# A two-layer attention backbone: transposes in place of diagonal products in the opening, six buffers for the modulation weights, and the opening left to the scheduler's order

## The chip, the cores and the metric

One NeuronCore of a Trainium2 chip; the other cores are not used. The metric is the device time of one execution in microseconds (us), the median of three runs.

The engines are called by the names of the profile: PE is TensorE (PEld its loading of weights), DVE is VectorE, ACT is ScalarE, POOL is GpSimd, and SP is the engine whose queue issues nearly all DMA transfers. Each engine takes its instructions in the order in which they stand in its own queue, and waits on semaphores for the others.

## The reference

One sequence of 1024 tokens `x` and 256 context tokens `ctx`, 1024 wide, in float32, go through two layers: windowed attention with sink logits, then multi-head latent attention. What matters here is the start of layer 0:

```
for i in range(DEPTH):
    shift_x, scale_x, gate_x = adaln(c, ada_w[i], ada_b[i])        # silu(cond) @ ada_w + bias, split in 3
    shift_c, scale_c, gate_c = adaln(c_ctx, ada_w[i], ada_b[i])
    hx = rms_norm(x, norm_g[i]) * (1.0 + scale_x[:, None]) + shift_x[:, None]
    hc = rms_norm(ctx, norm_g[i]) * (1.0 + scale_c) + shift_c
    ...
    q, k, v, g = jnp.split(h @ w_in, [...], axis=-1)               # layer 0, for hx and hc
    ...                                                            # attention, gate, output projection
    x = x + gate_x[:, None] * yx
return rms_norm(x, final_g)
```

So before the first projection can start, the modulation (shift and scale) must be computed from `ada_w`, 8 MB of it in this layer, every row of `x` and `ctx` must be normalised, and the result must stand with the channels on the partitions, since a product on PE sums over partitions.

## The kernel before

**Number format.** A float32 value is split into a high part (`hi`, rounded to the format that PE reads in one pass) and a low part (`lo = src - hi`); `split` makes both, the high part on ACT and the low part on DVE or POOL. A product is three matmuls (`mm3`, L126 to L128): high x high, low x high, high x low.

**Tiles.** The 1280 tokens (context first) are ten tiles of 128 rows (`x_load(i)`, i = 0 to 9), or five pairs p of 256. `h` is held transposed, `hT[p]`, channels on partitions: 8 chunks of 128 channels, high and low.

**The opening** (L656 to L856) does the following before the loop of projections.

- `ada_load(h, k)` (L671) loads 128 rows of `ada_w` for half h of the columns (512 of shift, 512 of scale): sixteen loads of 512 KB, through the ring of buffers `awr`. `ada_mm(h, k)` (L675) multiplies such a piece with `silu(c)` and sums in PSUM bank `PA`: two products with only two rows of output. `ada_cols(h)` copies the sums out (L678, on ACT), turns them into columns (L680) and adds bias and gain (L168, L171).
- `norm(i)`: sum of squares of a tile on ACT (L691), then mean, epsilon and the power -1/2 on POOL (L692, L693).
- `diag(i)` (L699, on DVE): a 128 x 128 diagonal matrix with the reciprocal root of each row.
- `turn(g)` (L711, on PE): a group g is one pair p and two of its 8 chunks (`parts[g]`; 20 groups, the first eight alternate between pairs 0 and 1). Four products of a 128 x 128 piece of the raw tile with the diagonal give the scaled piece, transposed, in one of four PSUM banks. In the profile each of these float32 products is two records.
- `h_part(g)`: modulation out of PSUM on DVE (L722, two instructions) and the high part on ACT (L723); `h_low(g)`: the low part on POOL or DVE (L728).
- `v_part(g)`: 12 matmuls (4 products) with the V columns of `w_in`, into `PB[:, 4 + p % 2]`; after the last group of a pair the V rows are stored (L744, L746).
- `w0_load`, `w0_cut`: the load (L752) and the split of the 1 MB of V columns. `fetch(1)` starts the next block of weights (L288), `cosa` and `sina` are loaded (L851, L852).

**What sets the order.** Before the opening the framework's scheduler orders each engine's queue by its own estimate of when an instruction can run. `tc.manual_schedule()` stops that: from where it is entered to where it is left, every queue has the order of the source. In the kernel before it is entered ahead of the opening, so opening and projections are in source order. In both kernels it is left behind the projections; the attention of layer 0 and layer 1 are ordered by the scheduler.

**Rings.** A `Ring` hands out the buffers of a list in turn. A load into a buffer waits until those that read its former content are done, and everything behind it in SP's queue waits with it.

**After the opening**: ten blocks of 256 columns of `w_in` for all tokens (`proj_t`), with the rest of the modulation computed on DVE beside it (`ada_vec`, L342 and L344, its pieces loaded at L323), then attention by units, output projection, and layer 1.

Of the kernel before, what the change touches and what calls it, by code (L numbers as in the profile page):

```python
# [12 lines left out]
AF = mybir.ActivationFunctionType  # L13
# [10 lines left out]
NP = TOK // 256  # L24
# [35 lines left out]
def kernel(ctx: ExitStack, tc: tile.TileContext, t, out, dbg=None):  # L60
# [591 lines left out]

    awr = Ring(F, [0, 4, 8, 12], 1024)
    xs = Ring(F, [16, 20, 24, 28], 1024)  # L656
    w0 = f_at(32, 8, 256)
    am = f_at(40, 512)
    dg = Ring(F, [42, 42.5, 43, 43.5], 128)
    junk = f_at(50, 512).bitcast(BF16)  # L660
    hr = Ring(F, [44, 46, 48, 32], 512)
    PA, PM = PB[:, 6, :], PB[:, 7, :]
    parts = [(p, b) for h in range(2) for p in range(2) for b in (2 * h, 2 * h + 1)]
    parts += [(p, b) for p in range(2, NP) for b in range(4)]
    NG = len(parts)
    aw, xn, hs = {}, {}, {}

    def ada_load(h, k):
        aw[h, k] = shp(awr.next(), 2, 512)
        src = t["ada_w"][0, k * 128 : k * 128 + 128, 0 : 2 * D].rearrange("p (a c) -> p a c", a=2)  # L670
        load(out=aw[h, k], in_=src[:, :, h * 512 : h * 512 + 512])  # L671

    def ada_mm(h, k):
        for a in range(2):
            nc.tensor.matmul(PA[32 * a : 32 * a + 2], sc[:, k, :], aw[h, k][:, a, :], start=k == 0, stop=k == 7)  # L675
# [9 lines left out]
    def x_load(i):  # L685
        xn[i] = [xs.next(), sm_ring()]
        load(out=xn[i][0], in_=src0(i))

    def norm(i):
        st = xn[i][1]  # L690
        nc.scalar.activation(junk, xn[i][0], AF.Square, accum_out=st[:, 0:1])  # L691
        nc.gpsimd.tensor_scalar(st[:, 1:2], st[:, 0:1], 1.0 / D, EPS, ALU.mult, ALU.add)  # L692
        nc.gpsimd.tensor_tensor(st[:, 2:3], st[:, 1:2], mhalf, ALU.pow)  # L693

    def diag(i):

        st = xn[i][1]
        xn[i][1] = dg.next()
        nc.vector.tensor_scalar_mul(xn[i][1], ident, st[:, 2:3])  # L699

    def bank(g):
        return shp(PB[:, g % 4, :], 2, 256)

    def turn(g):

        p, b = parts[g]
        for kk in range(2):
            for j in range(2):
                x, d = xn[2 * p + j]
                c0 = (2 * b + kk) * 128  # L710
                nc.tensor.matmul(  # L711
                    bank(g)[:, kk, j * 128 : j * 128 + 128], x[:, c0 : c0 + 128], d, start=True, stop=True
                )

    def h_part(g):
        p, b = parts[g]
        w = 1 if p == 0 else 0
        hs[g] = shp(hr.next(), 2, 256)
        for kk in range(2):
            k = 2 * b + kk  # L720
            sa, sb = ada0.A[:, k, w : w + 1], ada0.B[:, k, w : w + 1]
            nc.vector.tensor_scalar(hs[g][:, kk], bank(g)[:, kk], sa, sb, ALU.mult, ALU.add)  # L722
        nc.scalar.copy(hT[p][:, 0, 2 * b : 2 * b + 2, :], hs[g])  # L723
# [24 lines left out]
    wt[0] = r_at(wst[0], 2, 8, 256)  # L748

    def w0_load(i):  # L750
        ks = slice(4 * i, 4 * i + 4)
        load(out=w0[:, ks, :], in_=w_in[512 * i : 512 * i + 512, 1280:1536].rearrange("(k p) n -> p k n", p=128))  # L752

    def w0_cut(i):
        ks = slice(2 * i, 2 * i + 2)
        split(wt[0][:, 0, ks, :], wt[0][:, 1, ks, :], w0[:, ks, :], nc.vector if i % 2 else nc.gpsimd)


    in_order = tc.manual_schedule()
    in_order.__enter__()  # L760
    nc.vector.memset(PA[0:34], 0.0)
    ada_load(0, 0)
    load_small()
# [2 lines left out]
    x_load(0)  # L766
    x_load(1)
    ada_load(0, 3)
    ada_mm(0, 0)
    ada_load(0, 4)  # L770
    ada_mm(0, 1)
    ada_load(0, 5)
    w0_load(0)
    ada_mm(0, 2)
    ada_load(0, 6)
    for i in range(2):
        norm(i)
    for i in range(2):
        diag(i)
    ada_mm(0, 3)  # L780
    ada_load(0, 7)
    w0_cut(0)
    w0_cut(1)
    ada_mm(0, 4)
    ada_mm(0, 5)
    x_load(2)
    x_load(3)
    turn(0)
    turn(1)
    ada_mm(0, 6)  # L790
    ada_mm(0, 7)
    ada_load(1, 0)
    w0_load(1)
    for k in (1, 2, 3):
        ada_load(1, k)
    ada_cols(0)
    norm(2)
    h_part(0)
    norm(3)
    h_part(1)  # L800
    diag(2)
    diag(3)
    h_low(0, nc.gpsimd)
    turn(2)
    turn(3)
    ada_mm(1, 0)
    ada_load(1, 4)
    for g in (2, 3):
        h_part(g)
        h_low(g - 1, nc.gpsimd)  # L810
        turn(g + 2)
        v_part(g - 2)
        ada_mm(1, g - 1)
        ada_load(1, g + 3)
    h_low(3, nc.vector)
    turn(6)
    turn(7)
    v_part(2)
    ada_mm(1, 3)
    ada_load(1, 7)  # L820
    for i in range(4, 8):
        x_load(i)
    w0_cut(2)
    w0_cut(3)
    v_part(3)
    for k in range(4, 8):
        ada_mm(1, k)
    ada_cols(1)
    for g in range(4, NG + 2):
        if g < NG:  # L830
            h_part(g)
        p = (g + 4) // 4
        if g % 4 < 2 and p < NP:
            norm(2 * p + g % 4)
        if g % 4 == 2 and p < NP:
            diag(2 * p)
            diag(2 * p + 1)
        if 5 <= g <= NG:
            h_low(g - 1, nc.vector if g % 4 == 0 else nc.gpsimd)
        if 6 <= g < NG - 2:  # L840
            turn(g + 2)
        if g == 8:
            next_item()
            fetch(1)
        if g == 9:
            x_load(8)
            x_load(9)
        if g in (11, 13, 15):
            next_item()
        if g == 12:  # L850
            load(out=cosa, in_=t["cos_a"])  # L851
# [792 lines left out]
```

## Time and profile before

| | us |
|---|---|
| median of 3 runs | 1653.48 (1653.24 to 1655.42) |
| the profiled execution | 1653.19 |
| its span, first to last instruction | 1651.1 |
| PE busy | 1587.6 |
| DVE, ACT, POOL busy | 944.9, 802.0, 813.3 |
| first matmul | 6.22 |
| first h_part (L722) | 24.50 |
| last wait of the V product in the opening, ended at | 105.68 |

A matmul's row in the timeline is its start, its length with the drain behind it, the line and the shape; matmuls overlap, so the time that one takes from the next is the distance between two starts. What stands in brackets at the end of a row is how long the engine had been idle before it and who ended that. "PEclk" is the granted clock of PE, 1.00 being full speed.

### The profile page before, as it was taken

The numbers are of one execution on the slowest core, as the hardware profiler recorded it, in microseconds if no ns is written. First come the engines' busy times: TensorE is split into PE (matmuls) and PEld (weight loads), VectorE is DVE, ScalarE is ACT, GpSimd is POOL, SyncE is SP. The second block draws the span as 40 slices with busy tenths as digits, with TensorE's granted clock in tenths as the row PEclk, the third lists the DMA queues.
The fourth block names the chain that finished last, engine by engine and source line by source line (L and its number), as shares of the span: only waits on it lengthen the run. The fifth ranks groups of instructions, "written<-read, shape, count | busy, mean of one in ns | idle before, by whom it ended". The sixth has DMA issues, their size and how long they took to land.

```text
span 1651.1 us, 23676 instructions
## 1 busy us (share of the span) xinstructions
PE 1587.6 (96%) x8236; PEld 1224.5 (74%) x8236; DVE 944.9 (57%) x1722; ACT 802.0 (49%) x1713; POOL 813.3 (49%) x870
## 2 busy tenths in 40 slices
PE   6799999989999999998999999999999999999998
PEld 3588888777888888887987887565766756666687
DVE  2447768827767777768444106655455445455354
ACT  2321211328877777777323324555555555555421
POOL 2344536415544344444245521787676777668510
PEclk8799999999999999999999999999999999999999
DMA  7336454474433333326126722211111111122141
GB/s 257 137 100 201 139 177 166 137 226 133 120 107 90 94 93 94 92 93 198 52 66 241 236 80 80 75 54 40 41 39 36 45 33 42 45 80 69 47 159 65
DMA packets 122399, 176.74 MB, mean 107 GB/s; under 512 B 11420, under 2 KB 71452, under 8 KB 122280
## 3 DMA queue, kind: packets, MB, share of 16 engines
q1 hardware_dynamic: 115000, 164.31, 30.7%
q10 hardware_dynamic: 7280, 10.92, 2.1%
q8 instruction: 65, 1.06, 0.3%
q14 instruction: 54, 0.44, 0.1%
HBM read 129.04 MB, written 46.15 MB: 106 GB/s over the span
## 4 chain that ended last, share of the span: by engine, by line
PE 82%; DVE 5%; ACT 4%; issue 4%; POOL 3%; DMA 2%; ACTq 0%; POOLq 0%; SPq 0%; DVEq 0%
PE PB L126 17%; PE PB L128 17%; PE PB L127 17%; PE PB L1317 9%; PE PB L570 5%; PE PB L1283 4%; PE PB L560 4%; PE PB L533 2%; PE PB L534 2%; PE PB L711 1%; DMA arena_f<-ada_w 1%; DVE arena_f L344 1%; PE PB L675 1%; PE PB L1342 1%; ACT arena_f L1302 1%
## 5 line engine op out<-in xcount | busy, mean ns | idle before, releaser
L126 PE MATMUL PB<-arena_r 128*128 128x512 f32 (+3 forms) x1632 | 607.9, 373 | 4.4 <-ACT arena_r L205 2.1
L127 PE MATMUL PB<-arena_r 128*128 128x512 f32 (+3 forms) x1632 | 595.2, 365 | 1.0 <-POOL arena_r L728 1.0
L128 PE MATMUL PB<-arena_r 128*128 128x512 f32 (+3 forms) x1632 | 593.8, 365 | 0.2 <-DVE arena_r L122 0.2
L126 PEld LDWEIGHTS PB<-arena_r 128*128 128x128 f32 (+1 forms) x1632 | 309.9, 190 | 93.1 <-issue 32.9
L1309 POOL TENSOR_TENSOR arena_f<-arena_f 128x512 f32<-128x512 f32 x252 | 327.2, 1299 | 75.3 <-ACT arena_f L1302 60.1
L128 PEld LDWEIGHTS PB<-arena_r 128*128 128x128 f32 (+1 forms) x1632 | 308.9, 190 | 49.1 <-DVE arena_r L122 0.4
L127 PEld LDWEIGHTS PB<-arena_r 128*128 128x128 f32 (+1 forms) x1632 | 310.1, 190 | 41.8 <-POOL arena_r L728 1.2
L1287 DVE TENSOR_REDUCE arena_f<-PB 128x1 f32<-128x1280 f32 x128 | 190.4, 1488 | 105.0 <-PE PB L1283 102.5
L1302 ACT ACTIVATE arena_f<-PB 128x512 f32<-128x512 f32 x320 | 189.0, 598 | 125.1 <-PE PB L128 113.3
L122 DVE TENSOR_TENSOR arena_r<-PB,arena_r 128x512 fp32r<-128x512 f32 (+4 forms) x245 | 158.7, 655 | 125.9 <-ACT arena_r L121 124.1
L122 POOL TENSOR_TENSOR arena_r<-arena_f,arena_r 128x512 fp32r<-128x512 f32 x80 | 111.1, 1403 | 174.7 <-ACT arena_r L121 155.6
L121 ACT CAST arena_r<-PB 128x512 fp32r<-128x512 f32 (+4 forms) x245 | 135.5, 557 | 67.7 <-PE PB L560 39.1
L540 DVE CUSTOM_DVE_ANT_0 arena_f<-PB,arena_f,small 128x256 f32<-128x256 f32 (+1 forms) x288 | 145.3, 523 | 32.4 <-PE PB L534 25.3
L1317 PE MATMUL PB<-arena_f 128*64 128x512 f32 x640 | 157.1, 600 | 0.0
L541 ACT ACTIVATE arena_f<-arena_f,small 128x640 f32<-128x640 f32 (+2 forms) x160 | 118.9, 744 | 27.8 <-DVE small L540 26.9
L570 PE MATMUL PB<-arena_r 128*128 128x512 f32 x336 | 120.8, 436 | 4.5 <-ACT arena_f L581 4.1
L344 DVE SCALAR_TENSOR_TENSOR arena_f<-arena_f,small 128x512 f32<-128x512 f32 x98 | 114.9, 1217 | 3.0 <-DMA arena_f<-ada_w 2.7
L560 PE MATMUL PB<-ident,arena_f 128*128 128x128 f32 x672 | 104.9, 273 | 0.4 <-ACT arena_f L541 0.3
L1317 PEld LDWEIGHTS PB<-arena_f 128*64 128x64 f32 x640 | 43.5, 136 | 80.9 <-issue 79.5
L121 ACT CAST arena_r<-arena_f 128x512 fp32r<-128x512 f32 (+1 forms) x120 | 69.3, 607 | 69.9 <-DMA arena_f<-a_w_in 21.2
L1283 PE MATMUL PB<-arena_r 96*128 96x512 f32 (+1 forms) x384 | 99.7, 367 | 0.3 <-DVE arena_f L1287 0.2
L560 PEld LDWEIGHTS PB<-ident,arena_f 128*128 128x128 f32 x672 | 82.6, 140 | 15.0 <-ACT arena_f L541 1.5
(162 smaller groups left out, 1743.1 us busy)
## 6 DMA issues: line engine op xcount, KB each, us to landing
arena_r<-q_d SPq DMA_DIRECT2D x148, 128.0 KB, 2.8
arena_f<-ada_w SPq DMA_DIRECT2D x64, 256.0 KB, 3.6
arena_f<-a_w_in SPq DMA_DIRECT2D x36, 256.0 KB, 2.9
arena_f<-ada_w SPq DMA_DIRECT2D x16, 512.0 KB, 6.6
arena_f<-x SPq DMA_DIRECT2D x16, 512.0 KB, 4.4
q_d<-arena_f SPq DMA_DIRECT2D x16, 512.0 KB, 3.0
qn_d<-arena_f SPq DMA_DIRECT2D x16, 512.0 KB, 5.0
arena_r<-qn_d SPq DMA_DIRECT2D x32, 256.0 KB, 3.5
```

The source lines that it names most:

```text
L121: nc.scalar.copy(hi, src)
L122: (lo_eng or nc.vector).tensor_sub(lo, src, hi.bitcast(F32))
L126: nc.tensor.matmul(o, ah, bh, start=first, stop=False)
L127: nc.tensor.matmul(o, al, bh, start=False, stop=False)
L128: nc.tensor.matmul(o, ah, bl, start=False, stop=last)
L560: nc.tensor.transpose(pt[:, h, :], self.Ps[h][:, ci * 128 : ci * 128 + 128], ident)
L570: nc.tensor.matmul(self.pv, V[:, self.chunks[ci], self.g, :], PT[:, s], start=ci == 0 and s == 0, stop=ci == self.m - 1 and s == 1,)
L1283: nc.tensor.matmul(psm[:, n0 : n0 + n], self.qT[0:96, 0, b * 128 : b * 128 + 128], kt[0:96, 0, n0 : n0 + n], start=True, stop=True,)
L1287: nc.vector.reduce_max(self.mx[:, 96 + b : 97 + b], psm[:, 0:TOK], AX.X, negate=True)
L1302: nc.scalar.activation(E, S, AF.Exp)
L1309: eng.tensor_add(self.acc, self.acc, E)
L1317: nc.tensor.matmul(self.pv[p : p + 64], Vq[:, c, self.h % 4, :], self.E.pop(c), start=c < 2, stop=c >= NT - 2)
```

## The change

- `turn` makes a PE transpose of a piece of a tile (with the identity as the other operand) in place of a product with a diagonal; the tile itself is scaled before, in place, by `scale(i, eng)`: on DVE for eight tiles, on ACT for tiles 7 and 9. `diag` and its ring go.
- `awr` has six buffers for four. Room for them: the ring of x tiles moves, and the V columns of `w_in` are loaded in four pieces through a ring of two buffers (`w0r`) in place of two pieces into one area.
- The code of the opening is written in another order, and `tc.manual_schedule()` is entered only behind it, ahead of the loop of projections: the opening's queues have the scheduler's order.
- Behind the first four groups, the low parts of groups 9, 13 and 16 are made on DVE, in place of those of groups 7, 11, 15 and 19, and `fetch(1)` is called one step earlier.

The number of matmuls in the V product and in the modulation, and their operands, stay. Line numbers of the opening's functions fall by one (L711 is L710, L675 is L674, and so on), those behind it rise.

```diff
-    awr = Ring(F, [0, 4, 8, 12], 1024)
-    xs = Ring(F, [16, 20, 24, 28], 1024)
-    w0 = f_at(32, 8, 256)
-    am = f_at(40, 512)
-    dg = Ring(F, [42, 42.5, 43, 43.5], 128)
+    awr = Ring(F, [0, 4, 8, 12, 16, 20], 1024)
+    xs = Ring(F, [24, 28, 32, 36], 1024)
+    w0r = Ring(F, [40, 42], 512)
+    am = f_at(48, 512)
...
-    hr = Ring(F, [44, 46, 48, 32], 512)
+    hr = Ring(F, [44, 46, 40, 42], 512)
...
-    def diag(i):
-
-        st = xn[i][1]
-        xn[i][1] = dg.next()
-        nc.vector.tensor_scalar_mul(xn[i][1], ident, st[:, 2:3])
+    def scale(i, eng):
+        x, st = xn[i]
+        if eng is nc.scalar:
+            nc.scalar.activation(x, x, AF.Copy, scale=st[:, 2:3])
+        else:
+            eng.tensor_scalar_mul(x, x, st[:, 2:3])
...
-                x, d = xn[2 * p + j]
                 c0 = (2 * b + kk) * 128
-                nc.tensor.matmul(
-                    bank(g)[:, kk, j * 128 : j * 128 + 128], x[:, c0 : c0 + 128], d, start=True, stop=True
+                nc.tensor.transpose(
+                    bank(g)[:, kk, j * 128 : j * 128 + 128], xn[2 * p + j][0][:, c0 : c0 + 128], ident
                 )
...
     def w0_load(i):
-        ks = slice(4 * i, 4 * i + 4)
-        load(out=w0[:, ks, :], in_=w_in[512 * i : 512 * i + 512, 1280:1536].rearrange("(k p) n -> p k n", p=128))
+        w0[i] = shp(w0r.next(), 2, 256)
+        load(out=w0[i], in_=w_in[256 * i : 256 * i + 256, 1280:1536].rearrange("(k p) n -> p k n", p=128))
...
-    in_order = tc.manual_schedule()
-    in_order.__enter__()
     nc.vector.memset(PA[0:34], 0.0)
...
+    for i in range(2):
+        scale(i, nc.vector)
+    for i in (2, 3):
+        w0_load(i)
+        x_load(i)
+    for k in range(2):
+        ada_load(1, k)
     ada_mm(0, 4)
-    ada_mm(0, 5)
-    x_load(2)
-    x_load(3)
     turn(0)
     turn(1)
...
-        p = (g + 4) // 4
-        if g % 4 < 2 and p < NP:
-            norm(2 * p + g % 4)
-        if g % 4 == 2 and p < NP:
-            diag(2 * p)
-            diag(2 * p + 1)
+        if g == 4:
+            norm(4)
+            norm(5)
+        if g == 5:
+            scale(4, nc.vector)
+            scale(5, nc.vector)
+        if g in (7, 11):
+            norm(g - 1 if g < 8 else 8)
+        if g in (8, 12):
+            norm(7 if g < 10 else 9)
+            scale(6 if g < 10 else 8, nc.vector)
+        if g in (9, 13):
+            scale(7 if g < 10 else 9, nc.scalar)
         if 5 <= g <= NG:
-            h_low(g - 1, nc.vector if g % 4 == 0 else nc.gpsimd)
+            h_low(g - 1, nc.vector if g in (10, 14, 17) else nc.gpsimd)
...
-        if g == 8:
+        if g == 7:
             next_item()
             fetch(1)
...
     started = {0, 1}
+
+    in_order = tc.manual_schedule()
+    in_order.__enter__()
     for bi, gp, c in order:
```

Three places in the queues. PE, from the first modulation products (L675, L674 in the change) to the columns made of the first half (L680, L679), with the turns (L711, L710). Before:

```order
L675 MATMUL PB<-arena_f,small 2x512 x12
L711 MATMUL PB<-arena_f 128x128 x8
L675 MATMUL PB<-arena_f,small 2x512 x4
L680 MATMUL PB<-ident,arena_f 128x34 x4
L711 MATMUL PB<-arena_f 128x128 x8
```

Now:

```order
L674 MATMUL PB<-arena_f,small 2x512 x6
L710 MATMUL PB<-ident,arena_f 128x128 x2
L674 MATMUL PB<-arena_f,small 2x512 x2
L710 MATMUL PB<-ident,arena_f 128x128 x6
L674 MATMUL PB<-arena_f,small 2x512 x8
L679 MATMUL PB<-ident,arena_f 128x34 x4
L710 MATMUL PB<-ident,arena_f 128x128 x4
```

Turns 0 and 1 stand between the products of the third, fourth and fifth load, where they stood behind those of the sixth.

ACT, from the first copy of the modulation sums to the second (copy L678, L677 in the change; norm L691, L690; high part of h L723, L722; L121 is the high part of a piece of weights). Before:

```order
L678 COPY arena_f<-PB 34x512
L691 ACTIVATE arena_f,small<-arena_f 128x1024
L723 CAST arena_r<-arena_f 128x512
L691 ACTIVATE arena_f,small<-arena_f 128x1024
L723 CAST arena_r<-arena_f 128x512 x3
L121 CAST arena_r<-arena_f 128x512 x2
L678 COPY arena_f<-PB 34x512
```

Now, and what follows the second copy:

```order
L677 COPY arena_f<-PB 34x512
L690 ACTIVATE arena_f,small<-arena_f 128x1024
L121 CAST arena_r<-arena_f 128x512
L722 CAST arena_r<-arena_f 128x512
L690 ACTIVATE arena_f,small<-arena_f 128x1024
L722 CAST arena_r<-arena_f 128x512 x3
L690 ACTIVATE arena_f,small<-arena_f 128x1024
L677 COPY arena_f<-PB 34x512
L690 ACTIVATE arena_f,small<-arena_f 128x1024 x2
```

The norm of tile 4, the fifth, stands ahead of the second copy, and those of tiles 5 and 6 right behind it.

SP, from the last modulation loads of layer 0 (L671, L670 in the change) to the last x tiles (L687, L686); L288 are pieces of the next weight blocks, L851 and L852 (L859 and L860) the tables. Before:

```order
L671 DMA arena_f<-ada_w 128x2x512 x7
L687 DMA arena_f<-x 128x1024 x4
L288 DMA arena_f<-a_w_in 128x2x256 x3
L687 DMA arena_f<-x 128x1024 x2
L288 DMA arena_f<-a_w_in 128x2x256
L851 DMA arena_f<-cos_a 128x1024
L852 DMA arena_f<-sin_a 128x1024
```

Now:

```order
L670 DMA arena_f<-ada_w 128x2x512 x8
L686 DMA arena_f<-x 128x1024 x4
L288 DMA arena_f<-a_w_in 128x2x256 x3
L859 DMA arena_f<-cos_a 128x1024
L860 DMA arena_f<-sin_a 128x1024
L288 DMA arena_f<-a_w_in 128x2x256 x2
L686 DMA arena_f<-x 128x1024 x2
```

Tiles 8 and 9 stand behind the tables and two more pieces of weights.

More of the change, by code (lines that the diff above doesn't have):

```diff
@@ L665 @@
     NG = len(parts)
-    aw, xn, hs = {}, {}, {}
+    aw, xn, hs, w0 = {}, {}, {}, {}
     def ada_load(h, k):
@@ L750, in w0_load @@
     def w0_load(i):
-        ks = slice(4 * i, 4 * i + 4)
-        load(out=w0[:, ks, :], in_=w_in[512 * i : 512 * i + 512, 1280:1536].rearrange("(k p) n -> p k n", p=128))
+        w0[i] = shp(w0r.next(), 2, 256)
+        load(out=w0[i], in_=w_in[256 * i : 256 * i + 256, 1280:1536].rearrange("(k p) n -> p k n", p=128))
     def w0_cut(i):
         ks = slice(2 * i, 2 * i + 2)
-        split(wt[0][:, 0, ks, :], wt[0][:, 1, ks, :], w0[:, ks, :], nc.vector if i % 2 else nc.gpsimd)
-    in_order = tc.manual_schedule()
-    in_order.__enter__()
+        split(wt[0][:, 0, ks, :], wt[0][:, 1, ks, :], w0[i], nc.vector if i % 2 else nc.gpsimd)
     nc.vector.memset(PA[0:34], 0.0)
@@ L768 @@
     ada_load(0, 3)
[L769 to L772, printed above, removed]
     w0_load(0)
-    ada_mm(0, 2)
-    ada_load(0, 6)
+    w0_load(1)
+    for k in (4, 5):
+        ada_load(0, k)
+    for k in range(3):
+        ada_mm(0, k)
     for i in range(2):
         norm(i)
-    for i in range(2):
-        diag(i)
+    for k in (6, 7):
+        ada_load(0, k)
     ada_mm(0, 3)
-    ada_load(0, 7)
     w0_cut(0)
     w0_cut(1)
+    for i in range(2):
[5 more added lines that the diff above has]
+        ada_load(1, k)
     ada_mm(0, 4)
-    ada_mm(0, 5)
-    x_load(2)
-    x_load(3)
     turn(0)
     turn(1)
[L790 to L794, printed above, removed]
+    for k in (5, 6, 7):
+        ada_mm(0, k)
+    w0_cut(2)
+    w0_cut(3)
+    for k in range(2, 6):
         ada_load(1, k)
@@ L797 @@
     norm(2)
+    norm(3)
     h_part(0)
-    norm(3)
+    scale(2, nc.vector)
     h_part(1)
-    diag(2)
-    diag(3)
+    scale(3, nc.vector)
     h_low(0, nc.gpsimd)
+    h_low(1, nc.gpsimd)
+    ada_mm(1, 0)
+    ada_load(1, 6)
+    v_part(0)
+    ada_mm(1, 1)
+    ada_load(1, 7)
     turn(2)
     turn(3)
[L806 to L814, printed above, removed]
-    h_low(3, nc.vector)
+    ada_mm(1, 2)
+    h_part(2)
+    h_part(3)
+    h_low(2, nc.gpsimd)
+    h_low(3, nc.vector)
+    v_part(1)
+    ada_mm(1, 3)
+    turn(4)
+    turn(5)
+    ada_mm(1, 4)
+    v_part(2)
+    ada_mm(1, 5)
     turn(6)
     turn(7)
-    v_part(2)
-    ada_mm(1, 3)
-    ada_load(1, 7)
     for i in range(4, 8):
         x_load(i)
-    w0_cut(2)
-    w0_cut(3)
     v_part(3)
-    for k in range(4, 8):
-        ada_mm(1, k)
+    ada_mm(1, 6)
+    ada_mm(1, 7)
     ada_cols(1)
```

## The prediction

> **What bounds the kernel now.** I read the page first, then the opening stage by stage, then the waits of TensorE (PE) there, then the timeline at the places where it waits.
>
> The page's span, its PE row and the rows of forty slices (41.3 us each):
>
> ```profile
> span 1651.1 us, 23676 instructions
> PE 1587.6 (96%) x8236; PEld 1224.5 (74%) x8236; DVE 944.9 (57%) x1722; ACT 802.0 (49%) x1713; POOL 813.3 (49%) x870
> ...
> PE   6799999989999999998999999999999999999998
> ...
> PEclk8799999999999999999999999999999999999999
> ```
>
> PE is the bound everywhere but in the first three slices, and there alone the granted clock is low too. Now stages: PE's busy time with its instruction count, granted clock, DMA share and GB/s.
>
> ```profile
> 0.00:24.50 24.50, 14.01 (x52) 0.86 0.92 325
> 24.50:50.34 25.84, 21.66 (x128) 0.87 0.50 176
> 50.34:108.40 58.06, 42.34 (x292) 0.82 0.31 109
> 108.40:380.00 271.60, 263.47 (x1333) 0.99 0.53 171
> 500.00:520.00 20.00, 20.00 (x122) 1.00 0.48 146
> ```
>
> Up to 24.5 us the DMA engines are the limit (share 0.92). From there to 108.4, where the V product of the opening ends, they are half idle and PE is neither full nor at full clock. After 108.4 PE is full. So whatever moves the end of the opening moves the end of the kernel by as much; the order of the engines behind the opening is the same in both programs. What PE waits for before 108.4 (total, times, longest):
>
> ```profile
> PE PB L711 <- DVE arena_f L699: 18.6, 7, 4.6
> ...
> PE PB L127 <- POOL arena_r L728: 1.0, 1, 1.0
> ```
>
> The largest wait is the turning products (L711) for their diagonal matrix (L699). The four stretches in which PE ran at half clock, each behind such a wait:
>
> ```profile
> 26.60:33.00 6.40, 4.32 (x18) 0.50 0.33 121
> 53.80:63.40 9.60, 5.61 (x24) 0.50 0.21 69
> 74.00:80.60 6.60, 5.40 (x23) 0.50 0.03 6
> 91.50:94.70 3.20, 3.20 (x18) 0.53 0.00 0
> ```
>
> 18.5 us of busy time at about half clock: 9.3 us lost.
>
> **The change, part by part.** The first three rows are the end of the first set of modulation products and the copy that waits for it; then the first h_part; then one turn at full clock with the V product behind it; the rate of the loads from 10 to 20 us (385 GB/s) and PE's wait for the fourth load; last a group of four transposes in the attention stage, with what follows.
>
> ```profile
> 18.69 2.37 PE L711 MATMUL PB<-arena_f 128*128 128x128 f32 x16
> 20.99 1.89 PE L675 MATMUL PB<-arena_f,small 128*2 128x512 f32 x8
> 22.92 0.58 ACT L678 COPY arena_f<-PB 34x512 f32<-34x512 f32 x1 [4.11 <-PE PB L675]
> 24.50 1.90 DVE L722 TENSOR_SCALAR arena_f<-PB,small 128x256 f32<-128x256 f32 x4
> ...
> 33.83 1.16 PE L711 MATMUL PB<-arena_f 128*128 128x128 f32 x8
> 34.75 0.36 PE L126 MATMUL PB<-arena_r 128*128 128x256 f32 x1
> ...
> 10.00:20.00 10.00, 6.92 (x23) 1.85 (x21) 1.91 (x4) 3.43 (x6) 2.76 (x5) 0.66 1.04 385
> ...
> 13.47 5.29 PE L675 MATMUL PB<-arena_f,small 128*2 128x512 f32 x12 [3.08 <-DMA arena_f<-ada_w]
> ...
> 508.02 0.60 PE L560 MATMUL PB<-ident,arena_f 128*128 128x128 f32 x4
> 508.37 0.70 PE L570 MATMUL PB<-arena_r 128*128 128x512 f32 x2
> ```
>
> *First columns.* In PE's queue the first two turns moved from between the sixth and seventh load's products to between the third, fourth and fifth, where PE waits for loads anyway. Before, 2.3 us of turns stood ahead of the products of the last two loads, which had landed by then. As many bytes are queued ahead of the eighth load as before (half a weight block, two x tiles). The fourth landed at 13.47, five of 512 KB follow up to the eighth, at 385 GB/s 1.36 us each: 20.3. Its product takes 0.94 (two in 1.89), so the copy (L678) starts at 21.3 and h_part at 22.9 instead of 24.5: -1.6 us (between -2.3 and 0).
>
> *Turns.* Eight records from 33.83 to 34.75 are one turn: 0.92 us. Four transposes take 0.35 (508.02 to 508.37). 18 turns lie behind 24.5: 18 x 0.57 = -10.3 us. The price in the opening isn't seen; it lies between 0.35 and 0.92, so between -10.3 and 0. I take 0.35, the same form of instruction.
>
> The Trainium skill ("TensorE: Matmul & The Clock Gate", Part 4: PE-mode transpose) says that transpose mode does not count as PE activity for the clock gate. By that rule the new turns would help neither to reach nor to keep full clock; the attention row above (clock 1.00 at 500 to 520 with L560 in it) has too many other products to decide it. It is the third rival.
>
> *Scaling x itself.* The diagonal goes and x is scaled in place. The diagonal cost VectorE 0.28 to 1.31 us; scaling a 128x1024 tile has a twin in the next layer (L181). The rows give lowest, median and longest in ns; L723, L728 and L691 are the cast of h, its low half and the norm:
>
> ```profile
> L699 DVE TENSOR_SCALAR arena_f<-ident,small x10: 278/287/1308, 12.7 to 90.0; 128x128 f32<-128x128 f32 x10
> L181 DVE TENSOR_SCALAR arena_f<-arena_f,small x10: 740/753/1752, 742.8 to 787.5; 128x1024 f32<-128x1024 f32 x10
> ...
> L723 ACT CAST arena_r<-arena_f x20: 600/618/620, 25.5 to 104.6; 128x512 fp32r<-128x512 f32 x20
> L728 POOL TENSOR_TENSOR arena_r<-arena_f,arena_r x15: 1261/1265/1280, 28.1 to 104.4; 128x512 fp32r<-128x512 f32 x15
> L691 ACT ACTIVATE arena_f<-arena_f x10: 1051/1052/1056, 10.6 to 83.1; 128x1024 bf16<-128x1024 f32 x10
> ```
>
> So +0.45 us a tile, eight on VectorE and two on ScalarE (1.05 by L691). The waits above name VectorE for L699 alone, so this lies beside PE's work except where a turn waits for it.
>
> *Waits.* Behind 24.5 us PE waits for each new pair of x tiles and, at the end, for a low half: 18.6 + 1.0 = 19.6 us. The SP queue's rows, the second copy, one such wait in the chain that ended last, and the page's times to landing:
>
> ```profile
> 18.80 26.80 SPq L671 DMA_DIRECT2D arena_f<-ada_w  x7
> 45.70 1.85 SPq L687 DMA_DIRECT2D arena_f<-x  x4
> ...
> 50.39 0.58 ACT L678 COPY arena_f<-PB 34x512 f32<-34x512 f32 x1 [14.83 <-PE PB L675]
> ...
> 56.66 0.56 POOL small L693
> 57.25 1.29 DVE arena_f L699
> 58.58 1.65 PE PB L711 x6
> ...
> arena_f<-ada_w SPq DMA_DIRECT2D x16, 512.0 KB, 6.6
> arena_f<-x SPq DMA_DIRECT2D x16, 512.0 KB, 4.4
> ```
>
> The seven modulation loads hold SP's queue from 18.8 to 45.6, since four buffers come free only as their products run; the x tiles stand behind them. With six buffers only the last two loads wait for products of the second set. On ScalarE, the norm of the fifth x tile moved ahead of the second copy, and two more follow it at once. Walking the new order with these durations: x tile 4 is issued once turn 5 is done (near 34), lands 4.4 us later, and its norm ends near 39.7. The last product of the second set ends near 41: the first V product begins at 25.9 (22.9 and the 3.1 us below), then 4 V products of 1.42, 8 x 0.94 and 6 turns of 0.35. So the copy isn't held, with 1.4 us to spare.
>
> In SP's queue the last two x tiles moved behind two pieces of weights, which wait for POOL to cut earlier pieces (before, they stood ahead of the fourth piece).
>
> After, I expect: at the first V product the chain h_part 1.0, cast 0.6, POOL's low half 1.3, with the steps between 3.1 us of idle PE; at the fifth the same and 0.7 of norm arithmetic on POOL: 3.8; none for x tiles 6 and 7, scaled long before; x tiles 8 and 9 late by the SP rows. PE is at 41 + 1.6 (copy and columns) + 3.8 = 46.5 there and does eight groups of 1.42 + 0.35 up to about 61 or 62; the pieces ahead of tile 8 wait for POOL, which has a low half of 1.3 in each group too, to about 56; load 4.4, norm 1.2, arithmetic 0.7 and a scaling of 0.75 to 1.75 on each tile end near 65. 3.9 (0 to 8); and 0.6 at the end. 11.4 against 19.6: -8.2.
>
> *Clock.* Three waits are left that can drop it. The four stretches lost 2.3 us each on average; I take two and a half stretches: 5.8 against 9.3, -3.5 (between -9.3, never at half, and +33, always at half, the third rival).
>
> *The rest.* Products of the second set (8) and V products (20 groups) stay; the six buffers alone issue nothing new; w0 in four loads for two is two more SP issues. The 0.9 DMA share before 24.5 covers them.
>
> Sum: -1.6 - 10.3 - 8.2 - 3.5 = -23.6, and the V product's end near 84.5. The walk through the new order row by row, where products of the second set also fill waits, puts it some 3 us earlier; I take -25, between the two. The profiled execution took 1653.19 us (2.1 around its span) and the median 1653.48, 0.3 above; 1653.5 - 25 = **1628.5 us**.
>
> **Rivals.** *Late tiles.* If loads take 6.6 us from issue (the page's row for 512 KB of ada_w) instead of 4.4, the copy is held by 0.8 us, tile 8 comes 2.2 later, two scalings on the path take 1.75 for 0.75 beside POOL's work (+2), and the weights ahead of tile 8, whose cuts wait in POOL's queue, may cost 3 more. Together +8: about 1637. For it: SP's order; against it: the DMA share is only 0.3 to 0.5 then.
>
> *A warmer, shorter opening.* No half clock at all (another -5.8) and x tile 8 in time (-3.9): about 1619. Against: each of the four stretches at half clock lies behind a wait for a new pair, and three waits are left.
>
> *The clock stays down (the other side).* If an opening with transposes in a fifth of each group's time never earns full clock, everything on PE behind 22.9 doubles: V products 240 x 0.119 = 28.5 (nine steps from 105.90 to 106.97, below), second set 8 x 0.94 = 7.5, transposes 6.3: 42 us more, less the 5.8 that I counted, +36: 1628.5 + 36 = about 1664, slower by 11. It turns slower once 25/36, 70%, of that work is at half. Against it: V products are 1.42 of each 1.77 us of a group, and before, PE came back to full clock after 3.2 to 5.6 us of busy time.
>
> ```profile
> 105.90 0.28 PE L128 MATMUL PB<-arena_r 128*128 128x256 f32 x1
> ...
> 106.97 0.28 PE L128 MATMUL PB<-arena_r 128*128 128x256 f32 x1
> ```
>
> *Nothing.* The opening is bound by its loads: 26 of 512 KB at 1.4 us and some small ones are over near 50 us, well ahead of 84. Only a wait that I don't see could make it so.
>
> **How the numbers follow.** Forecast 0.72 (1620 to 1635), late tiles 0.14, warmer 0.07, clock down 0.04, nothing 0.03. The range leaves out the far ends of late tiles, the clock case and nothing: 1619 to 1638. 0.2%, 3.3 us, is about what a measurement of this kernel can tell from no change. Faster 0.94 (the first three and a quarter of the clock case), same 0.03, slower 0.03.
>
> **What would show it.** First h_part near 22.9; turns of four records with 0.35 to the next product; the V product's end near 84 instead of 108; no wait for the third pair of x tiles, and one of about 4 us near 62 behind the load of x tile 8; behind the opening every stage as long as before. It is wrong if the granted clock is near 0.5 through the V products, if ScalarE holds the second copy behind a norm, or if the projections behind the opening begin to wait for weights.

## The result, and the profile after

The changed kernel took 1632.92 us in the median (1630.86 to 1634.04, four runs), the kernel before 1653.36 (1651.42 to 1655.42, four runs): a ratio of 0.9876, 95% interval 0.9863 to 0.9888, 20.4 us faster. Timed again later beside the last experiments it took 1631.87, a ratio of 0.987 (0.9856 to 0.9883). The profiled execution took 1630.86 us.

Span, TensorE's (PE's) busy row and the forty slices of the page after:

```profile
span 1628.6 us, 23522 instructions
PE 1577.6 (97%) x8156; PEld 1213.2 (74%) x8156; DVE 947.7 (58%) x1719; ACT 803.8 (49%) x1715; POOL 815.5 (50%) x871
...
PE   6899999989999999999999999999999999999998
...
PEclk8999999989999999999999999999999999999999
```

The span is 22.5 us shorter; only the first slice is still below nine tenths by much. The stages after: length, PE's busy time and instruction count, granted clock, DMA share, GB/s.

```profile
0.00:22.90 22.90, 13.17 (x44) 0.93 0.92 324
22.90:48.00 25.10, 20.60 (x109) 0.86 0.77 274
48.00:84.50 36.50, 31.56 (x240) 0.91 0.35 123
84.50:356.10 271.60, 264.21 (x1328) 0.98 0.54 171
```

The third stage, from the second set of columns to the end of the V product, took 58.06 us before with 15.7 us of idle PE; it takes 36.5 with 4.9. The two ahead of it are only 2.3 us shorter together (48.0 for 50.34). The V product's end is read from the first shuffle behind it (L431, before and after), which came 12.17 us after it before (120.57, 108.40):

```profile
L431 DVE STREAM_SHUFFLE arena_f<-PB x20: 734/736/743, 120.6 to 314.6; 128x512 f32<-128x512 f32 x20
```

```profile
L431 DVE STREAM_SHUFFLE arena_f<-PB x20: 733/735/744, 96.7 to 290.7; 128x512 f32<-128x512 f32 x20
```

All twenty come 23.9 us earlier, so the opening ends at 84.5, as the prediction's sum had it. What PE still waits for up to 95 us:

```profile
PE PB L674 <- DMA arena_f<-ada_w: 6.4, 3, 5.7
PE PB L710 <- DVE arena_f L721: 3.6, 3, 1.5
PE PB L710 <- DVE arena_f L699: 3.3, 3, 2.1
PE PB L710 <- ACT arena_f L697: 2.3, 1, 2.3
PE PB L127 <- POOL arena_r L727: 2.2, 2, 1.1
```

The 18.6 us for the diagonals of new tiles (L699 before) have become 3.3 + 2.3 us for their scaling (L699 and L697 now). At about half clock PE ran in three stretches, two of them behind the first columns:

```profile
15.50:18.80 3.30, 3.30 (x12) 0.55 1.05 383
25.40:32.90 7.50, 6.38 (x26) 0.55 0.88 318
49.40:56.00 6.60, 5.50 (x25) 0.50 0.34 128
```

Behind the opening a little was given back. The first transposes of the attention (L560) came 23.1 us earlier, the last exponentials (L1302 before, L1313 after) 22.5. The first fence is before, the second after:

```profile
L560 PEld LDWEIGHTS PB<-ident,arena_f x672: 137/140/144, 383.8 to 734.9; 128*128 128x128 f32 x168
...
L1302 ACT ACTIVATE arena_f<-PB x320: 587/598/612, 1024.9 to 1563.0; 128x512 f32<-128x512 f32 x160
```

```profile
L560 PEld LDWEIGHTS PB<-ident,arena_f x672: 137/140/144, 360.7 to 711.8; 128*128 128x128 f32 x168
...
L1313 ACT ACTIVATE arena_f<-PB x320: 586/597/607, 1002.8 to 1540.5; 128x512 f32<-128x512 f32 x160
```

### The profile page after: what moved, and what is told of

It is laid out like the page before. It is cut to its first block, busy times and chain, and to the rows that moved or that the text cites. A ratio compares the mean times of both kernels' runs of the same rounds, so it can differ in the third digit from the quotient of the medians.

```text
span 1628.6 us, 23522 instructions
## 1 busy us (share of the span) xinstructions
PE 1577.6 (97%) x8156; PEld 1213.2 (74%) x8156; DVE 947.7 (58%) x1719; ACT 803.8 (49%) x1715; POOL 815.5 (50%) x871
## 4 chain that ended last, share of the span: by engine, by line
PE 82%; ACT 4%; DVE 4%; issue 3%; DMA 3%; POOL 3%; SPq 0%; ACTq 0%; POOLq 0%; DVEq 0%
PE PB L126 18%; PE PB L128 17%; PE PB L127 17%; PE PB L1328 9%; PE PB L570 5%; PE PB L1294 4%; PE PB L560 4%; PE PB L533 2%; PE PB L534 2%; DMA arena_f<-a_w_in 1%; PE PB L1353 1%; DVE arena_f L344 1%; ACT arena_f L581 1%; ACT arena_f L1313 1%; DMA arena_f<-x 1%
## 5 line engine op out<-in xcount | busy, mean ns | idle before, releaser
L1313 ACT ACTIVATE arena_f<-PB 128x512 f32<-128x512 f32 x320 | 189.0, 597 | 125.2 <-PE PB L128 112.8
L121 ACT CAST arena_r<-PB 128x512 fp32r<-128x512 f32 (+4 forms) x245 | 135.4, 557 | 68.1 <-PE PB L560 39.3
L540 DVE CUSTOM_DVE_ANT_0 arena_f<-PB,arena_f,small 128x256 f32<-128x256 f32 (+1 forms) x288 | 145.4, 523 | 32.1 <-PE PB L534 25.3
L121 ACT CAST arena_r<-arena_f 128x512 fp32r<-128x512 f32 (+1 forms) x120 | 69.7, 608 | 76.8 <-DMA arena_f<-a_w_in 26.4
L560 PE MATMUL PB<-ident,arena_f 128*128 128x128 f32 x672 | 104.9, 273 | 0.5 <-ACT arena_f L541 0.3
L560 PEld LDWEIGHTS PB<-ident,arena_f 128*128 128x128 f32 x672 | 82.6, 140 | 15.0 <-ACT arena_f L541 1.5
```

The source lines that it names most:

```text
L560: nc.tensor.transpose(pt[:, h, :], self.Ps[h][:, ci * 128 : ci * 128 + 128], ident)
L1313: nc.scalar.activation(E, S, AF.Exp)
```

## The experiments

The sum came out; whether its reasons did was open. The change has three parts: transposes with x scaled in place (T), the scheduler's order for the opening (S), and six modulation buffers with the loads written in another order (B). My theory was the prediction's: the largest share, some 10 us, is T, and the waits go because of B and of the order. The rival: the order S does nearly all, since what PE waits for is other engines' queues, and shorter turns only make it wait longer.

### One part undone, or one part alone

**The change without T** (diagonal products back; the diagonal is rounded to the format of the high parts, which costs the same instructions but gives up accuracy; that the rounding alone sets its output apart is not shown).

```diff
-            eng.tensor_scalar_mul(x, x, st[:, 2:3])
+            eng.tensor_scalar_mul(d, ident, st[:, 2:3])
...
-                nc.tensor.transpose(
+                nc.tensor.matmul(
```

> The change with the products with a diagonal back in place of the transposes (the diagonal rounded to the high part's format, and kept where K will stand later; six buffers, loads and the scheduler's order stay). If the shorter turns are PE time on the path, as the prediction has it (18 turns, 0.57 us each), the V product ends 9 to 11 us later than with the change (near 94 instead of 84.5) and the time is about 1642. If the turns lie beside waits and the gain comes from loads and order, it ends less than 4 us later, about 1635.

Measured: 1637.54 us, ratio 0.9911 (0.9896 to 0.9926): 4.6 us slower than the change's 1632.92, or 5.8 by the ratios to the kernel before. This lies between the two theories.

**The change without S** (the source's order held from the start of the opening).

```diff
+    in_order = tc.manual_schedule()
+    in_order.__enter__()
     nc.vector.memset(PA[0:34], 0.0)
```

> The change with the order of its source held from the start of the opening, so the scheduler orders nothing there. If transposes and six buffers carry the gain, it stands within 3 us of the change (1630 to 1636). If the scheduler's order carries a good part, it is 5 us or more slower than the change (1638 and up).

Measured: 1649.35 us, ratio 0.9983 (0.9973 to 0.9992): 16.4 us slower than the change. Six buffers, transposes and the new source order together are worth 3 us without the scheduler. In its trace the scales of tiles 4 and 5 still cost PE 7.0 us and those of tiles 6 to 9 nothing, but the waits for GpSimd's low halves, 1.0 us before, have grown:

```profile
PE PB L127 <- POOL arena_r L727: 11.7, 5, 3.9
```

**T alone** in the old kernel.

```diff
-                nc.tensor.matmul(
-                    bank(g)[:, kk, j * 128 : j * 128 + 128], x[:, c0 : c0 + 128], d, start=True, stop=True
+                nc.tensor.transpose(
+                    bank(g)[:, kk, j * 128 : j * 128 + 128], xn[2 * p + j][0][:, c0 : c0 + 128], ident
```

> The kernel before, with transposes and scaling in place and nothing else of the change. If turns are PE time on the path: 18 x 0.57 = 10 us less, minus up to 2 us where a scaling of 0.75 to 1.75 us stands in a wait in place of a diagonal: 1643 to 1646, with the four waits for new x tiles still there. If they lie beside waits: 1650 or more.

Measured: 1648.23 us, ratio 0.9974 (0.9965 to 0.9984), 4.3 us faster than before, between the two expectations. Its largest wait shows where part of the saved work went, 22.2 us for scales where it was 18.6 for diagonals:

```profile
PE PB L709 <- DVE arena_f L698: 22.2, 8, 5.0
```

**S alone** in the old kernel (the source's order held only behind the opening; diagonals and four buffers stay).

```diff
-    in_order = tc.manual_schedule()
-    in_order.__enter__()
     nc.vector.memset(PA[0:34], 0.0)
...
     started = {0, 1}
+    in_order = tc.manual_schedule()
+    in_order.__enter__()
```

> The kernel before, with the source's order held only behind the opening and nothing else of the change (four buffers, products with a diagonal). If the buffers are what makes the x tiles late, SP's queue is still held by the modulation loads and the gain is 0 to 5 us (1648 to 1653). If the order alone takes the waits away: 8 us or more (1645 or less).

Measured: 1634.34 us, ratio 0.9888 (0.9871 to 0.9904): 18.2 us faster, nearly the whole gain. With the kernel before on the same chip at 1652.57, T is worth 4.3 and S 18.2.

**T and S without B** (the edits of the last two runs together).

> The old kernel with two of the change's three parts: the transposes, and the scheduler's order for the opening; its four modulation buffers and its source order stay. The scheduler alone measured 1634.34, the change 1631.87 on this chip beside a before of 1653.2. Theory A (buffers and loads written in another order bring nothing of their own; the change's last 2.5 us over the scheduler alone are the transposes): 1630 to 1634, first shuffle 95 to 99. Rival (the transposes give their time back as waits, as they did in the source order, and only earlier loads turn them into time): 1634 to 1638, first shuffle 100 or later.

Measured: 1631.9 us beside a before of 1654.05, ratio 0.9868 (0.9851 to 0.9884): the change's time. So B brings nothing of its own; T and S are the change. Without T, B even cost time: S with B (the first run above) took 1637.54 us, S alone 1634.34.

**The change with four buffers.**

```diff
-    awr = Ring(F, [0, 4, 8, 12, 16, 20], 1024)
+    awr = Ring(F, [0, 4, 8, 12], 1024)
```

> The change with four modulation buffers instead of six. Theory A (the buffers matter little, since the old kernel in the scheduler's order came within 1.4 us of the change with four): 1632 to 1636. Rival, the prediction's view (the six buffers bring the second set of columns forward, and with it the wait at the fifth V product): 3.8 us and more slower, 1636.5 to 1640, second set of columns at 49 us or later instead of 45.7.

Measured: 1642.27 us, ratio 0.9933 (0.992 to 0.9947), 10.4 slower than the change on that chip, and slower than both theories had it; the second set of products ended at 54.4 us, not 45.7. But this is no fair test of the buffers. PE's queue has the first two turns ahead of all modulation products here, so the first product starts at 16.86 us (5.75 in the change), and three more loads than there are buffers have been issued by 14.2:

```profile
9.49 4.68 SPq L670 DMA_DIRECT2D arena_f<-ada_w  x3
...
13.03 0.69 PE L710 MATMUL PB<-ident,arena_f 128*128 128x128 f32 x2 [13.03 <-DVE arena_f L699]
...
16.86 4.44 PE L674 MATMUL PB<-arena_f,small 128*2 128x512 f32 x16
```

Those three loads go into buffers whose pieces PE has not read yet, and the kernel's output is not the reference's; that the one causes the other is likely, but not shown. So whether the new order of loads needs its six buffers stays open; with the old order four do as well (the run before).

One row of each trace, from the start to the end of the V product, tells what the parts do (length, PE's busy time, count, clock, DMA share, GB/s): before, T, S, T with S, the change.

```profile
0.00:108.40 108.40, 78.01 (x471) 0.84 0.50 174
```

```profile
0.00:101.67 101.67, 66.16 (x391) 0.85 0.54 185
```

```profile
0.00:87.98 87.98, 71.58 (x471) 0.94 0.62 214
```

```profile
0.00:86.10 86.10, 66.39 (x391) 0.90 0.64 218
```

```profile
0.00:84.50 84.50, 65.33 (x392) 0.90 0.63 222
```

Length less busy is idle PE: 30.4 before, 35.5 with T, 16.4 with S, 19.7 with both, 19.2 in the change. T takes 11.9 us off the busy time in the source's order, and 5.1 come back as idle; in the scheduler's order it takes 5.2 off, with a lower clock beside it (0.90 for 0.94), and 3.3 come back. S takes 14.0 us of idle away, and 6.4 of busy time: the instructions are the same (471) and the clock is 0.94 for 0.84.

### Why the order matters

In the old kernel SP's queue issued the fifth x tile at 45.70 us, behind seven modulation loads. With S alone, and four buffers still, the x loads stand between the modulation loads from 33.67 us on, and on ScalarE two norms stand ahead of the copy that waits for PE's last modulation product:

```profile
33.67 0.34 SPq L687 DMA_DIRECT2D arena_f<-x  x1
...
39.28 1.06 ACT L691 ACTIVATE arena_f<-arena_f 128x1024 bf16<-128x1024 f32 x1 [8.02 <-DMA arena_f<-x]
...
43.18 1.06 ACT L691 ACTIVATE arena_f<-arena_f 128x1024 bf16<-128x1024 f32 x1 [2.75 <-DMA arena_f<-x]
...
45.79 0.58 ACT L678 COPY arena_f<-PB 34x512 f32<-34x512 f32 x1 [1.47 <-PE PB L675]
```

The later pairs had stood in the wrong place too. In the old kernel x tiles 6 and 7 were issued by 47.6 us, but their norms stood behind a cast of V rows that waited for PE, and PE then waited for their diagonals; with S alone these norms run at 46.28 and 47.46, right behind the copy. Before:

```profile
65.67 0.65 ACT L744 CAST arena_r<-PB 128x256 fp32r<-128x256 f32 x2 [5.59 <-PE PB L128]
...
68.57 1.05 ACT L691 ACTIVATE arena_f<-arena_f 128x1024 bf16<-128x1024 f32 x1
...
74.78 0.80 PE L711 MATMUL PB<-arena_f 128*128 128x128 f32 x2 [4.49 <-DVE arena_f L699]
```

Six buffers and the new order of loads get the x tiles out early as well: the change without S issues them from 39.29 us, and they land about 4 us later. But there the copy comes first, waits 10.25 us for PE, and the norm comes some 7 us after its tile:

```profile
39.29 5.36 SPq L686 DMA_DIRECT2D arena_f<-x  x4
...
47.21 0.58 ACT L677 COPY arena_f<-PB 34x512 f32<-34x512 f32 x1 [10.25 <-PE PB L674]
...
50.42 1.05 ACT L690 ACTIVATE arena_f<-arena_f 128x1024 bf16<-128x1024 f32 x1
```

GpSimd shows the same in that kernel. Its low half (L727) stood behind the arithmetic of a norm (L691), which waited for a square on ScalarE, which itself stood behind a cast of h that waited, through VectorE, for PE; PE waited 3.85 us for that low half:

```profile
66.24 0.19 POOL L691 TENSOR_SCALAR small<-small 128x1 f32<-128x1 f32 x1 [4.86 <-ACT arena_f L690]
...
67.03 2.50 POOL L727 TENSOR_TENSOR arena_r<-arena_f,arena_r 128x512 fp32r<-128x512 f32 x2
```

**Two moves by hand.** The change with the source's order held, the norms and scales of tiles 4 and 5 ahead of the second set of columns, and in the loop the low half ahead of the norms.

```diff
+    norm(4)
+    norm(5)
+    scale(4, nc.vector)
+    scale(5, nc.vector)
     ada_cols(1)
     for g in range(4, NG + 2):
         if g < NG:
             h_part(g)
-        if g == 4:
-            norm(4)
-            norm(5)
-        if g == 5:
-            scale(4, nc.vector)
-            scale(5, nc.vector)
+        if 5 <= g <= NG:
+            h_low(g - 1, nc.vector if g in (10, 14, 17) else nc.gpsimd)
         if g in (7, 11):
...
-        if 5 <= g <= NG:
-            h_low(g - 1, nc.vector if g in (10, 14, 17) else nc.gpsimd)
```

> The changed kernel's source with its order held from the start (measured 1649.35), and two hand moves in that order: the norms and scales of x tiles 4 and 5 stand ahead of the second set of columns, and in the loop over groups the low part of the last group stands ahead of the norms. Theory A (what the scheduler saves is that GpSimd and ScalarE don't hold a due low part or a norm behind work that waits for TensorE): TensorE's waits of 5.04 and 1.99 us for the scales of tiles 4 and 5 fall to some 1.5 us, the waits for GpSimd's low parts from 11.7 to 5 to 8 us, in all 8 to 11 us off: 1638 to 1641. Rival (the gain lies in TensorE's own order, the pieces of the modulation products put between the halves of V products): 2 us off at most, 1647 to 1650.

Measured: 1639.66 us, ratio 0.9912 (0.9897 to 0.9927): 9.7 us off the 1649.35, as the theory had it. The wait for the scales of tiles 4 and 5 is gone, though one of 2.4 us for tile 7's, on ScalarE, is new; the waits for low halves were 11.7 us and are 8.4, where the theory had 5 to 8:

```profile
PE PB L127 <- POOL arena_r L727: 8.4, 4, 4.9
```

So over half of what the scheduler saves in this source comes from two moves in the queues of ScalarE, GpSimd and VectorE; the other 6.7 us were not taken apart. The wait of 4.9 left is GpSimd's order again: at 69.5 us it cuts three pieces of weights (4.16 us) ahead of the low half.

### What is left: clock and late tiles

**Nine products, or 22 transposes, of the identity behind each set of columns**, where PE waits 1.49 us; nobody reads them. They tell whether transposes keep the clock.

```diff
         ada0.set_cols(m[:, :, 0:2], 0, h)
+        for _ in range(22):
+            nc.tensor.transpose(PM[:, 0:128], ident, ident)
```

> Nine 128x128 float32 products of the identity with itself stand on TensorE behind each set of columns, where it otherwise waits for the first columns of h (1.49 us each time); their results are read by nobody. In the changed kernel TensorE runs at half clock from 25.4 to 32.9 and from 49.4 to 56.0 us, each stretch shortly behind such a wait. Theory A (an idle TensorE loses its clock, any work keeps it): the fill of some 2 us covers the first wait of each place, may hold the transposes of h up by up to 0.9 us, and both half-clock stretches go or start later, when the wait of 1.1 us for the low part still stands: 3 to 6 us off, 1627 to 1630, granted clock near 1.00 from 22.9 to 48 (0.86 in the changed kernel). Theory B (the clock follows the demand of the last few us, the transposes and the 1.1 us wait behind them are enough to lose it): the half-clock stretches stay, 1632 to 1635.

> The same place as in the run with products, filled with 22 transposes of the identity (0.09 us each at full clock, about 2 us) instead of nine products. Theory A (any work of TensorE keeps the clock): the same as with products, 1627 to 1630 with no half-clock stretch behind the first columns. Theory C (transposes don't count as activity, as the Trainium skill, page TensorE: Matmul & The Clock Gate, states of a transpose mode): the half-clock stretches of 25 to 33 and 49 to 56 us stay or start earlier, 1632 to 1636, while the run with products loses them. If both runs keep their stretches neither is shown.

Measured: 1630.43 us, ratio 0.9854 (0.9838 to 0.9871) with products, 1630.1, ratio 0.9851 (0.9837 to 0.9866) with transposes; neither time is clearly told apart from the change's. The clocks are. The scheduler, which orders these openings too, also put PE's first turns elsewhere in the two kernels, so they differ in more than the fill. With transposes (18 to 65 us, and behind that):

```profile
18.00:65.00 47.00, 41.85 (x298) 1.00 0.75 271
65.00:72.00 7.00, 3.67 (x16) 0.51 0.21 81
```

With products, the fill itself and what follows:

```profile
23.26:27.90 4.64, 4.64 (x26) 0.63 1.05 388
28.00:68.00 40.00, 34.97 (x248) 1.00 0.66 230
```

Both lost the stretch at 49 us; with products 4 us at half clock stayed behind the first columns, with transposes none. So transposes keep the clock here at least as well as products. The rule of the Trainium skill ("TensorE: Matmul & The Clock Gate", Part 4: PE-mode transpose) that a transpose doesn't count as PE-busy the same way is not borne out by these rows, which are float32 where the page measured bf16: 2.4 us of nothing but transposes, from 22.8 to 25.2, left the clock at 1.00. Why the time hardly moved shows on ScalarE, with the fill of transposes: PE, now early, met the x tiles 8 and 9 late, waited 3.68 and 1.39 us for their scales, and lost its clock there.

```profile
63.04 1.06 ACT L692 ACTIVATE arena_f<-arena_f 128x1024 bf16<-128x1024 f32 x1 [4.88 <-DMA arena_f<-x]
```

**x tiles 8 and 9 loaded with tiles 4 to 7** in the change.

```diff
-    xs = Ring(F, [24, 28, 32, 36], 1024)
+    xs = Ring(F, [24, 28, 32, 36, 16, 20], 1024)
...
-    for i in range(4, 8):
+    for i in range(4, 10):
         x_load(i)
```

> The changed kernel with six x buffers (the two more lie where the last two of the modulation buffers were) and the loads of x tiles 8 and 9 moved right behind those of tiles 4 to 7. In the changed kernel x tile 8 reaches the chip at 64.90 us, and TensorE waits 0.68 and 2.28 us for its scale and that of tile 9 at 69 to 72 us. Theory A (that wait is set by the load alone): both go, 2.5 to 3.2 us off, 1629.7 to 1630.5, and the first shuffle comes 2.5 to 3.2 us earlier than at 96.66. Rival: ScalarE and VectorE are behind as well at 65 to 70 us (their columns and low parts stand ahead of the scales), and half or more of the wait stays: 1631.5 to 1633.

Measured: 1631.36 us, ratio 0.9862 (0.9847 to 0.9877), not told apart from the change; the first shuffle came 0.5 us earlier (96.1), which is less than the change's own two traces differ (96.7 and 97.4). The wait of 2.96 us shrank to 0.4, but waits for GpSimd's low halves and others of 0.3 to 0.6 us came in its place. GpSimd is full there:

```profile
66.00:72.00 6.00, 5.84 (x7) 1.00 0.54 162
```

**Both edits together.**

> Both edits: the 22 transposes behind each set of columns, and the x tiles 8 and 9 loaded with tiles 4 to 7 into two more buffers. With the fill alone TensorE kept its full clock from 18 to 65 us, caught up with the load of x tile 8 (ScalarE waited 4.88 us for it, to 63.04), waited 3.68 and 1.39 us for the scales of tiles 8 and 9 and ran at half clock from 65.4 to 72. With the early load alone the wait shrank to 0.38 us, but the half-clock stretches of 25 and 49 us stood. Theory A (one gain was eaten by the other's wait): both waits go, 5 us, and the half-clock stretch behind them, some 3 us: first shuffle near 87 to 90 us instead of 95.5, time 1622 to 1626. Rival (what TensorE gains in the opening is given back behind it, as 1.4 us of the change's were): first shuffle as early, time 1627 to 1630.

> The change itself, to stand beside the others of this call on the same chip: 1630.5 to 1634, by the 1632.92 and the spread of its first runs.

Measured: 1626.22 us (1625.39 to 1626.89), ratio 0.9835 (0.9821 to 0.9848); the change beside it 1631.87. That is 5.6 us better than the change, and the best version here. PE keeps its clock from 18 us to the end of the V product:

```profile
18.00:80.20 62.20, 56.27 (x409) 1.00 0.60 212
```

The first shuffle is at 92.4 us, not at the 87 to 90 expected: 14.3 us of idle are left, 10.0 of them up to 24 us, most of that at the loads; behind it the largest wait is 2.1 for GpSimd's low halves.

In all these kernels the span less the first shuffle lies between 1530.5 us (before) and 1532.3: what differs is the opening, and what is given back behind it is 2 us at most. In the change 0.8 of the 1.4 us are gone by the first transposes of the attention; the cause stays open.

## Why the prediction was right or wrong

The range held the time, and the sign was given a chance of 0.94. The forecast of 1628.5 was 4.4 us low. That the parts summed to what the first shuffle shows was partly luck: the shorter turns were worth less than their term, and the order more.

*The sum, -23.6.* The first shuffle shows -23.9. Busy PE fell by 12.7 us (78.01 to 65.33) where turns and clock were to give 13.8, idle PE by 11.2 (30.4 to 19.2) where first columns and waits were to give 9.8.

*First columns, -1.6.* The first h_part started at 23.36 us, 1.1 earlier than before:

```profile
23.36 1.45 DVE L721 TENSOR_SCALAR arena_f<-PB,small 128x256 f32<-128x256 f32 x3
```

*Turns, 0.35 each.* A turn's four transposes take 0.36 us to the next product, a whole group 1.88 (56.76 to 58.64), not 1.77, since twelve products take 1.52, not 1.42:

```profile
56.76 0.60 PE L710 MATMUL PB<-ident,arena_f 128*128 128x128 f32 x4
57.12 0.36 PE L126 MATMUL PB<-arena_r 128*128 128x256 f32 x1
...
58.64 0.60 PE L710 MATMUL PB<-ident,arena_f 128*128 128x128 f32 x4
```

As busy time the term came out (11.9 us in T alone, by 20 turns, some of them at half clock). The price of 0.92 was read from one early turn, though; six later ones before the change took 0.81 at full clock, such as

```profile
96.44 1.05 PE L711 MATMUL PB<-arena_f 128*128 128x128 f32 x8
97.25 0.36 PE L126 MATMUL PB<-arena_r 128*128 128x256 f32 x1
```

As a reason the term failed: "18 x 0.57 = -10.3 us" counted the shorter turns as if they all lay on the path, but in T alone 8 waits for the scales of the next tiles stand among them, and T brings no scale earlier. T is worth 4.3 us alone and 2 to 6 in the scheduler's order.

*Waits, -8.2.* The places were right: at the fifth V product PE waits 0.7, 1.5, 0.6 and 1.1 us, for tiles 8 and 9 0.7 and 2.3 (forecast 3.9), none for 6 and 7. The credit was half wrong: the norm ahead of the copy does it, as the prediction's sentence on ScalarE has it, and the scheduler does that with four buffers too, and brings the norms of tiles 6 and 7 forward as well. The second set ended at 45.7 us, not near 41, mostly because half clock fell on it (2.9 us, which the walk left to the clock's term), the first columns were 0.5 late and a V product takes 0.1 longer; the norm of x tile 4 (41.13) was still ahead of the copy.

*Clock, -3.5.* Behind the first columns two stretches lost 6.38 x 0.45 + 5.50 x 0.50 = 5.6 us; 5.8 was forecast, from two and a half. The wait for tiles 8 and 9 cost no clock in this trace; in the change's second profile one did, from 70.8 to 74 us.

*From -23.6 to -25.* The walk row by row, which I let pull the sum down by 1.4, was wrong by nearly the whole 3 us. Another 1.4 was given back behind the opening (23.9 to 22.5), where I had let the two programs run alike. Most of the rest is that the profiled execution, 1630.86, was the fastest of its four runs.

*Rivals.* Tiles 8 and 9 cost 2.96 us, not the late tiles' +8, though one scaling did take 1.78 us beside GpSimd's work; the clock did not stay down, and "nothing" fell with the first trace. "Warmer" needed both its conditions: that is the last experiment. At 1626.22 it is 7 us above the price of 1619, which started from a forecast 4.4 too low and had no wait on GpSimd (2.1 us).

## What to carry to other kernels

Split a stage into busy and idle time of the engine that bounds it, and for each edit ask which of the two it takes away: a cheaper instruction in front of a wait in part only makes the wait longer (11.9 us of work saved, 5.1 of it back as idle, 4.3 us of time in the median). Where an engine waits, look in the queue of the one it waits for: a copy or an arithmetic step that itself waits for the bound engine, standing ahead of work that is ready, cost more here than all the turns: two moves gave 9.7 us. Two edits whose times can hardly be told from the change's (a fill for the clock, an earlier load) were worth 5.6 us together. That each uncovers the other's wait is what the traces say: the first shuffle at 95.5 and 96.1 us with one, at 92.4 with both, against 96.7 and 97.4 in the change's two traces. The times alone don't show it: by their ratios the edits gave some 3 and 1 us, within the spread, and could nearly add up to the 5.6.

## What the runs showed of the hardware

In the change TensorE lost its clock at 23 to 25 us, though from 18 us on no wait had been longer than 1.5 us. In the first trace it idled 0.75 and 1.49 us up to 24.41, and the granted clock fell near 25.3, while it worked; a wait of 1.12 us came only after that. In the change's second trace the clock fell near 22.9, behind 0.83 us of idle and 0.3 us into a wait of 1.49. With the fill of 22 transposes 0.83 and 0.33 us of idle came before, and the clock stayed at 1.00. With nine float32 products it was 0.84 and 0.33 us, and the clock was at half from about 23.9 to 27.9, while the products ran. What tells these apart was not settled.

A float32 transpose of 128x128 took 0.09 us from one to the next at full clock (four in 0.36), a float32 product with a diagonal 0.20 to 0.23 (four in 0.81 to 0.92).
